# One line of a mixer's hand-written order: three state products and two ropes put elsewhere in the program

## The chip, the cores and the metric

The kernel runs on one core of one Trainium2 chip. A core has five engines, each with a queue of its own that it works through in order: TensorE (PE; its weight loads are shown apart as PEld), VectorE (DVE), ScalarE (ACT), GpSimd (POOL) and SyncE (SP), which here issues the transfers. The engines wait for one another only through semaphores. The metric is device time in microseconds (us), lower is better: 1969.81 us is the median of three runs (1968.73 to 1970.2).

## The reference, cut to what matters

Two transformer blocks run one after the other on 512 tokens of width 1024. The first is a feed-forward layer, a mixer, another feed-forward layer and a gate; the second is two layers of a recurrent mixer. The change lies in the first block's mixer alone:

```
z = rmsnorm(h, norm_mix) @ w_in
q, kc, vc, ksl, vsl, kw, vw, g, u = split(z)
q, kc, ksl, kw = rope(q), rope(kc), rope(ksl), rope(kw)
o_nsa = nsa_attention(q, kc, vc, ksl, vsl, kw, vw, sigmoid(g), ...)   # compresses kc and vc, then attends
o_s5  = s5_mixer(u, ...)                                              # a complex linear recurrence over time
h = h + concat(o_nsa, o_s5) @ w_out
```

`rope` turns pairs of values by a position's angle. `s5_mixer` runs a state-space recurrence in 32 groups of 16 channels.

## The kernel before, in words

**Weights.** All weight matrices stream from memory as one sequence of chunks of eight 128x128 blocks (class `Stream`). A chunk is loaded by SP into `wstage` (3 buffers, L82), copied by ACT into a rounded high part `whi` (L98), and DVE forms the rest as the low part `wlo` (L108). A product of a block is three matmuls (`mm3`, L145 to L147): high x high, high x input's low part, low x high. So the third matmul of a chunk is the first that needs `wlo`. The code asks for parts ahead: at the second block of a chunk it issues the `whi` of the chunk after next, at the fifth block the `wlo` of the chunk after next. Since every engine works in order, where this asking stands in the program decides what is queued ahead of it.

**The mixer's middle part.** The string `ORDER` (L668) is a list of steps that `act` carries out one by one:

- `p0` to `p7`: one projection each, 24 matmuls of 128x512, one chunk of weights (`proj`). The results of p2 and p3 are keys, those of p4 to p7 queries.
- `r0` to `r7`: what follows a projection. For all but r1 this is `rope`: four ACT copies of a quarter each out of the PSUM bank (L638), one DVE product out of the same bank (L639), and put off into the list `todo` two more DVE operations (L642, L643) and, for keys, the splitting into parts (L828, L829, and two POOL copies L830, L832).
- `v0` to `v3`: eight small matmuls into a PSUM bank (L762, "state product"), a POOL product (L765), and two put-off steps `turn` and `back`, put at the front of `todo`: the state-space chain on DVE, L772 to L784, whose fourth operation is a scan. `back` also issues the loads of the tables of the next state product (L706, L709).
- `y0` to `y3`: first everything in `todo` is emitted, then 16 small matmuls (L797, L798; L798 reads the chain's result `s5w`), ACT copy and square (L801, L652); a gelu on DVE and ACT (L655, L656, L657, L660) and its write to memory are put off into `todo`.
- `b0`, `b1`: DVE and ACT gather windows for the compression (L854 to L858); `c0` to `c7`: a quarter each of two compressions, eight matmuls of 128x256 and a whole chunk of weights in about 1 us; `t`: a transpose and a small gelu; `u`: transfers; `xN`: emit N put-off steps.

A projection emits one put-off step after every second block. So what a `v` or `r` puts off is emitted on DVE and ACT in the midst of the next projection, and the request for `wlo` at the fifth block falls between such steps.

**Banks.** Projections and state products take PSUM banks in turn from two pairs, `pa` and `pb`. A bank is free again when what reads it (L639, L772 and L774, or L950) has run.

Names used below: "chunk of p4" is the chunk of weights that projection p4 multiplies by; "chain 2" is the DVE chain of v2.

Of the kernel before, what the change touches and what calls it, by code (L numbers as in the profile page):

```python
# [664 lines left out]


PROJ = [("w_kc", 0), ("w_vc", 0), ("w_ksl", 0), ("w_kw", 0)] + [("w_q", m) for m in range(4)]
ORDER = "p0 u v0 p1 r0 r1 p2 x2 b0 y0 p3 v1 c0 r2 p4 y1 c1 v2 x2 r3 c2 r4 b1 c3 p5 y2 p6 t v3 c4 r5 p7 r6 r7 y3 c5 c6 c7"  # L668


ATT = "c0 q0 S00 D00 c1 S01 c2 T000 D01 T001 T002 S10 T010 T012 D10 c3 S11 T011 D11 T101 q1 c4 V0 T100 T102 S20 c5 D20 T110 T111 S21 T112 D21 c6 c7 V1 T201 T200 T202 S30 T210 T211 D30 T212 S31 D31 V2 y0 q2 y1 T300 T301 T302 S40 T311 T312 D40 y2 T310 S41 D41 V3 T400 T401 y3 T402 S50 T411 D50 T410 T412 S51 D51 q3 g0 V4 T500 T501 S60 T502 T511 T512 D60 T510 S61 D61 V5 g1 T601 T600 T602 S70 T611 T612 D70 T610 S71 D71 g2 T700 T702 V6 T710 T712 T711 T701 g3 V7"
# [2 lines left out]
def mixer(k, xs, norm, ins, scr, on_tile):  # L674
    nc, v = k.nc, k.nc.vector
    with ExitStack() as outer:
# [45 lines left out]
        def pump(n=1):  # L722
            for _ in range(n):
                if todo:
                    todo.pop(0)()
# [217 lines left out]
        def act(s):  # L943
            kind, n = s[0], int(s[1:] or 0)
            if kind == "p":
                C["ps", n] = proj(*PROJ[n])
            elif kind == "r":
                name, m = PROJ[n]
                if name == "w_vc":
                    v.tensor_mul(kvc[1], C["ps", n], norm.row)  # L950
                elif name == "w_q":
                    roped(C["ps", n], q[m], scale=0.125)
                else:
                    roped(C["ps", n], *((kvc[0],) if name == "w_kc" else (None, keys(int(name == "w_kw")))))
            elif kind == "u":
                u_write(3)
                u_read(1)
            elif kind == "y":
                step(n)
            elif kind == "v":  # L960
                s5_v(n)
            elif kind == "b":
                drain()
                B[n] = cmp_blocks(n)
            elif kind == "c":
                x, j = divmod(n, 4)
                C[x] = cmp_h(x, B[x], ("cmp_wk1", "cmp_wv1")[x], range(4 * j, 4 * j + 4), C.get(x))
            elif kind == "t":
                C["g"] = cmp_t(0, C[0])
            elif kind == "x":  # L970
                pump(n)
        for s in ORDER.split():
            act(s)
# [1347 lines left out]
```

## Time and profile before

| | |
|---|---|
| median of 3 runs | 1969.81 us (1968.73 to 1970.2) |
| profiled execution | 1971.62 us, of which the span is 1969.9 us |
| PE busy | 1925.6 us, 98% of the span, 9336 matmuls |
| DVE busy | 1334.8 us, 68% |
| ACT busy | 830.7 us, 42% |
| POOL busy | 157.0 us, 8% |
| load of a weight chunk | 512 KB, 3.6 us median from issue to landing, 304 of them |

The span is what the trace covers. Busy shares are averages over very different stages. The stretch that the change touches lies from about 430 to 505 us; in it the granted TensorE clock (PEclk, 1.00 is 2.4 GHz, 0.50 is 1.2 GHz) isn't always full. A row of the timeline gives the start, the duration, the engine, the line, what it writes and reads, how many, and in brackets the engine's idle time before it and who ended that.

### The profile page before, as it was taken

How to read it: one execution, taken by the hardware profiler on the slowest of the kernel's cores; microseconds unless marked ns; L12 is line 12 of the kernel's file. 1: busy time of each engine (PE TensorE's matmuls, PEld its weight loads, DVE VectorE, ACT ScalarE, POOL GpSimd, SP SyncE). 2: the span in 40 equal slices, each digit the busy share in tenths (PEclk: the TensorE clock that was granted, in tenths of full speed). 3: DMA queues.
4: the chain of work that ended last, by engine and by line, in shares of the span. 5: the costliest groups of instructions: out<-in, count | busy, mean ns of one | idle time of the engine just before them, and what ended most of it. 6: DMA issues, size and time to landing. Idle time of an engine off the chain costs nothing.

```text
span 1969.9 us, 24779 instructions
## 1 busy us (share of the span) xinstructions
PE 1925.6 (98%) x9336; PEld 1577.9 (80%) x9336; DVE 1334.8 (68%) x2189; ACT 830.7 (42%) x1252; POOL 157.0 (8%) x217
## 2 busy tenths in 40 slices
PE   8999999997999999999999999999999999999997
PEld 6888888886867888888888877888888877888886
DVE  7766666768665575666666786887774775877743
ACT  5323232435555432232234455545442455555431
POOL 1000000111144000000001100111000000101001
PEclk9999999998899999999999999999999999999999
DMA  5334445366300365656543423222343233232241
GB/s 181 100 114 156 148 150 162 116 213 187 113 1 24 102 224 183 203 174 209 172 148 99 126 86 129 75 76 75 96 149 119 86 129 97 75 92 90 75 149 55
DMA packets 102553, 244.29 MB, mean 124 GB/s; under 512 B 24601, under 2 KB 37657, under 8 KB 102433
## 3 DMA queue, kind: packets, MB, share of 16 engines
q1 hardware_dynamic: 101744, 242.01, 38.7%
q8 instruction: 73, 1.20, 0.2%
q10 hardware_dynamic: 688, 0.70, 0.1%
q14 instruction: 48, 0.39, 0.1%
HBM read 220.38 MB, written 21.10 MB: 123 GB/s over the span
## 4 chain that ended last, share of the span: by engine, by line
PE 56%; DVE 7%; ACT 3%; issue 1%; POOL 0%; DVEq 0%; ACTq 0%
PE pbsecond L145 3%; PE pbsecond L147 3%; PE pbsecond L146 3%; PE pasecond L146 3%; PE pasecond L147 3%; PE pasecond L145 3%; PE pbhead L145 2%; PE pbhead L146 2%; PE pbhead L147 2%; PE pahead L147 2%; PE pahead L145 2%; PE pahead L146 2%; PE paout L145 2%; DVE wlo L108 2%; PE paout L147 2%; PE paout L146 2%
## 5 line engine op out<-in xcount | busy, mean ns | idle before, releaser
L108 DVE TENSOR_TENSOR wlo<-wstage,whi 128x1024 fp32r<-128x1024 f32 (+1 forms) x305 | 380.1, 1253 | 71.5 <-ACT whi L98 71.0
L98 ACT ACTIVATE whi<-wstage 128x1024 fp32r<-128x1024 f32 (+1 forms) x306 | 313.9, 1044 | 114.2 <-DMA wstage<-in_wpack_dram 26.0
L303 ACT ACTIVATE t<-t 128x512 f32<-128x512 f32 x44 | 27.9, 634 | 166.1 <-DVE t L302 166.1
L145 PE MATMUL pahead<-xnh,whi 128*128 128x512 f32 x208 | 83.3, 400 | 0.0
L147 PE MATMUL pahead<-xnh,wlo 128*128 128x512 f32 x208 | 81.3, 391 | 0.9 <-DVE wlo L108 0.9
L177 POOL TENSOR_TENSOR nacc<-nacc,nsq 128x512 f32<-128x512 f32 x20 | 27.2, 1365 | 681.5 <-ACT nsq L169 681.5
L146 PE MATMUL pahead<-xnl,whi 128*128 128x512 f32 x208 | 81.0, 390 | 0.0
L145 PE MATMUL pbhead<-xnh,whi 128*128 128x512 f32 x192 | 77.7, 405 | 1.7 <-DVE zs L1581 1.7
L145 PE MATMUL pbfirst<-xnh,whi 128*128 128x512 f32 x176 | 70.8, 402 | 7.9 <-ACT whi L98 6.5
L1571 DVE SCALAR_TENSOR_TENSOR conv<-cpad,vec,conv 128x512 f32<-128x512 f32 x96 | 72.2, 752 | 5.9 <-DVE conv L1569 0.5
L146 PE MATMUL pbhead<-xnl,whi 128*128 128x512 f32 x192 | 76.0, 396 | 0.0
L147 PE MATMUL pbhead<-xnh,wlo 128*128 128x512 f32 x192 | 75.9, 395 | 0.0
L146 PE MATMUL pbfirst<-xnl,whi 128*128 128x512 f32 x176 | 69.8, 397 | 0.0
L147 PE MATMUL pbfirst<-xnh,wlo 128*128 128x512 f32 x176 | 69.5, 395 | 0.0
L145 PE MATMUL pbsecond<-xnh,whi 128*128 128x512 f32 x176 | 68.9, 392 | 0.0
L145 PE MATMUL pasecond<-xnh,whi 128*128 128x512 f32 x176 | 68.8, 391 | 0.0
L145 PE MATMUL pafirst<-xnh,whi 128*128 128x512 f32 x176 | 68.7, 390 | 0.0
L147 PE MATMUL pafirst<-xnh,wlo 128*128 128x512 f32 x176 | 68.6, 390 | 0.0
L147 PE MATMUL pbsecond<-xnh,wlo 128*128 128x512 f32 x176 | 68.6, 390 | 0.0
L146 PE MATMUL pbsecond<-xnl,whi 128*128 128x512 f32 x176 | 68.5, 389 | 0.0
L147 PE MATMUL pasecond<-xnh,wlo 128*128 128x512 f32 x176 | 68.5, 389 | 0.0
L146 PE MATMUL pafirst<-xnl,whi 128*128 128x512 f32 x176 | 68.5, 389 | 0.0
(775 smaller groups left out, 5251.8 us busy)
## 6 DMA issues: line engine op xcount, KB each, us to landing
wstage<-in_wpack_dram SPq DMA_DIRECT2D x304, 512.0 KB, 3.6
adaw<-in_wada_dram SPq DMA_DIRECT2D x48, 512.0 KB, 4.5
adaw<-in_wshift_dram SPq DMA_DIRECT2D x8, 512.0 KB, 4.9
scr_v<-vv SPq DMA_DIRECT2D x16, 256.0 KB, 2.0
vr<-scr_v SPq DMA_DIRECT2D x16, 256.0 KB, 4.6
xr<-scr_x SPq DMA_DIRECT2D x16, 256.0 KB, 5.6
h<-in_xT_dram SPq DMA_DIRECT2D x8, 256.0 KB, 6.4
s5vw<-scr_wq SPq DMA_DIRECT2D x64, 32.0 KB, 2.1
```

The costliest lines, as they stand in the source:

```text
L98: k.nc.scalar.activation(self.hi[c][:, s], self.stage[c][:, s], AF.Copy)
L108: eng.tensor_sub(self.lo[c][:, s], self.stage[c][:, s], self.hi[c][:, s].bitcast(F32))
L145: mm(ps, w[0], x[0], start=start, stop=False)
L146: mm(ps, w[0], x[1], start=False, stop=False)
L147: mm(ps, w[1], x[0], start=False, stop=stop)
L177: k.nc.gpsimd.tensor_add(self.acc[1], self.acc[1], sq)
L303: nc.scalar.activation(t1, t1, AF.Silu)
L1571: v.scalar_tensor_tensor(c, xp[:, 1 + j:1 + j + T], w(j), c, op0=OP.mult, op1=OP.add)
```

## The change

Only the order string differs. Three state products and two ropes move:

```
-ORDER = "p0 u v0 p1 r0 r1 p2 x2 b0 y0 p3 v1 c0 r2 p4 y1 c1 v2 x2 r3 c2 r4 b1 c3 p5 y2 p6 t v3 c4 r5 p7 r6 r7 y3 c5 c6 c7"
+ORDER = "p0 u v0 p1 r0 r1 p2 x2 b0 y0 v1 p3 c0 r2 p4 y1 r3 c1 v2 r4 x2 c2 b1 c3 p5 y2 v3 p6 t c4 r5 p7 r6 r7 y3 c5 c6 c7"
```

- v1 goes ahead of p3 (was behind it), v3 ahead of p6 (was behind p6 and t).
- r3 goes ahead of c1 and v2, r4 ahead of the two put-off steps (`x2`) that are chain 2.

On SP the table loads that chain 1 issues (L706, L709, the second behind chain 1's reads of the old table) now stand ahead of one weight load and of the write of y0, where they stood behind both; POOL's order is unchanged. The amount of work is the same; the banks are handed out in another sequence (p3 now takes `pa`, v1 `pb`).

On DVE, behind the compression windows of b0 (the last of them is L858) and up to p4's low part: the difference, + for the order now and - for the order before.

```order
+L772 TENSOR_TENSOR s5r_3737<-pbmix,s5R 128x512
+L774 TENSOR_TENSOR s5r_3738<-pbmix,s5R 64x512 x2
+L775 TENSOR_TENSOR s5r_3737<-s5r_3737,s5r_3738 128x512
+L776 SCALAR_TENSOR_TENSOR s5r_3738<-s5rho,s5r_3737 128x512
+L781 TENSOR_TENSOR s5w_3736<-s5r_3738,s5R 128x8x63
+L783 TENSOR_TENSOR s5r_3737<-s5r_3738,s5R 64x512 x2
+L784 TENSOR_TENSOR s5w_3736<-s5w_3736,s5r_3737 128x8x63
+L108 TENSOR_TENSOR wlo<-wstage,whi 128x1024
 L655 TENSOR_SCALAR s5gw<-s5gw 128x512
 L656 TENSOR_TENSOR s5gw<-s5gw,s5yg 128x512
 L660 SCALAR_TENSOR_TENSOR s5yg<-s5gw,s5yg 128x512
-L108 TENSOR_TENSOR wlo<-wstage,whi 128x1024
```

Chain 1 (L772 to L784) now stands ahead of the low part of p4's chunk and of the gelu of y0; before, both stood ahead of the chain. In the same way chain 3 now stands ahead of the gelu of y2 and the low part of p7's chunk.

On ACT, behind y1 (L801 and L652): r3 and r4 are the four-copy groups L638; the first L98 is the high part of c3's chunk, the second that of p5's.

```order
 L801 ACTIVATE s5yg<-pc 128x512
 L652 ACTIVATE s5gw<-s5yg 128x512
+L638 ACTIVATE ropeb<-pamix 32x512 x4
 L98 ACTIVATE whi<-wstage 128x1024
 L638 ACTIVATE ropeb<-pbmix 32x512 x4
 L98 ACTIVATE whi<-wstage 128x1024
-L638 ACTIVATE ropeb<-pbmix 32x512 x4
 L657 ACTIVATE s5gw<-s5gw 128x512
```

Both groups moved one place forward: r3's copies are ahead of c3's high part, r4's ahead of p5's.

On DVE in the same place: the end of chain 2 as it stood, and what now stands ahead of it. The L108 with a + and the one behind the first L639 are low parts of c2's and c3's chunk, in that order.

```order
-L781 TENSOR_TENSOR s5w_3916<-s5r_3918,s5R 128x8x63
-L783 TENSOR_TENSOR s5r_3917<-s5r_3918,s5R 64x512 x2
-L784 TENSOR_TENSOR s5w_3916<-s5w_3916,s5r_3917 128x8x63
-L639 SCALAR_TENSOR_TENSOR ropeo<-pbmix,ropet 128x512
+L108 TENSOR_TENSOR wlo<-wstage,whi 128x1024
+L639 SCALAR_TENSOR_TENSOR ropeo<-pamix,ropet 128x512
 L108 TENSOR_TENSOR wlo<-wstage,whi 128x1024
 L639 SCALAR_TENSOR_TENSOR q_3314<-pbmix,ropet 128x512
+L772 TENSOR_TENSOR s5r_3924<-pamix,s5R 128x512
+L774 TENSOR_TENSOR s5r_3925<-pamix,s5R 64x512 x2
+L775 TENSOR_TENSOR s5r_3924<-s5r_3924,s5r_3925 128x512
+L776 SCALAR_TENSOR_TENSOR s5r_3925<-s5rho,s5r_3924 128x512
```

The first operations of r3 and r4 (both L639) moved ahead of chain 2; the low part of p5's chunk follows chain 2 directly, as before except for the L639 of r3 that stood between.

## Rows read from the trace of the kernel before

**Rows 1.** Waits of PE in the mixer: who for whom, total us, times, longest.
```profile
PE pbmix L145 <- DVE ropeo L639: 5.9, 1, 5.9
PE pc L798 <- issue: 4.1, 2, 2.6
PE pamix L147 <- DVE wlo L108: 1.7, 1, 1.7
```

**Rows 2.** Stretches: length, busy PE, PEld, DVE, ACT, POOL, PEclk, DMA, GB/s.
```profile
444.00:457.00 13.00, 11.53 (x71) 11.30 (x71) 9.81 (x13) 6.14 (x10) 3.65 (x4) 0.74 0.60 179
503.00:517.00 14.00, 13.97 (x109) 13.80 (x110) 9.52 (x17) 5.98 (x10) 0.00 (x0) 1.00 0.68 198
```

**Rows 3.** Timeline of DVE from b0 to c7's low part.
```profile
434.35 0.67 DVE L858 TENSOR_TENSOR cAh<-cA,cAh 128x496 fp32r<-128x496 f32 x1 [0.69 <-ACT cAh L857]
...
438.10 1.22 DVE L108 TENSOR_TENSOR wlo<-wstage,whi 128x1024 fp32r<-128x1024 f32 x1
439.24 0.69 DVE L772 TENSOR_TENSOR s5r<-pamix,s5R 128x512 f32<-128x512 f32 x1
...
446.13 1.22 DVE L108 TENSOR_TENSOR wlo<-wstage,whi 128x1024 fp32r<-128x1024 f32 x1
...
454.23 1.23 DVE L108 TENSOR_TENSOR wlo<-wstage,whi 128x1024 fp32r<-128x1024 f32 x1 [2.02 <-ACT whi L98]
455.82 0.69 DVE L772 TENSOR_TENSOR s5r<-pamix,s5R 128x512 f32<-128x512 f32 x1 [0.36 <-PE pamix L762]
...
463.32 1.22 DVE L108 TENSOR_TENSOR wlo<-wstage,whi 128x1024 fp32r<-128x1024 f32 x1
...
465.05 0.42 DVE L655 TENSOR_SCALAR s5gw<-s5gw 128x512 f32<-128x512 f32 x1
...
480.93 0.68 DVE L858 TENSOR_TENSOR cAh<-cA,cAh 128x496 fp32r<-128x496 f32 x1 [0.69 <-ACT cAh L857]
482.08 0.43 DVE L655 TENSOR_SCALAR s5gw<-s5gw 128x512 f32<-128x512 f32 x1 [0.47 <-ACT s5gw L652]
...
484.55 1.22 DVE L108 TENSOR_TENSOR wlo<-wstage,whi 128x1024 fp32r<-128x1024 f32 x1
...
497.90 1.28 DVE L639 SCALAR_TENSOR_TENSOR q<-pamix,ropet 128x512 f32<-128x512 f32 x2
...
501.76 3.49 DVE L108 TENSOR_TENSOR wlo<-wstage,whi 128x1024 fp32r<-128x1024 f32 x3
```

**Rows 4.** Timeline of PE: p4, y1, c1; p5, y2, p6; p7; c7.
```profile
439.37 0.50 PE L147 MATMUL pbmix<-xnh,wlo 128*128 128x512 f32 x1
...
444.52 0.33 PE L797 MATMUL pc<-U,s5T 128*128 128x64 f32 x2
...
451.71 0.55 PE L871 MATMUL pc<-whi,cAh 128*124 128x256 f32 x1
...
464.59 0.79 PE L147 MATMUL pbmix<-xnh,wlo 128*128 128x512 f32 x1
...
471.28 0.33 PE L797 MATMUL pc<-U,s5T 128*128 128x64 f32 x2
...
474.77 0.48 PE L145 MATMUL pamix<-xnh,whi 128*128 128x512 f32 x1
...
485.82 0.50 PE L147 MATMUL pamix<-xnh,wlo 128*128 128x512 f32 x1 [1.68 <-DVE wlo L108]
...
503.03 0.38 PE L872 MATMUL pc<-wlo,cAh 128*124 128x256 f32 x1 [0.37 <-DVE wlo L108]
```

**Rows 5.** Timeline of ACT: after y1, and the high part of c5's chunk.
```profile
453.16 1.04 ACT L98 ACTIVATE whi<-wstage 128x1024 fp32r<-128x1024 f32 x1
454.22 2.40 ACT L638 ACTIVATE ropeb<-pbmix 32x512 f32<-32x512 f32 x4
...
486.48 1.05 ACT L98 ACTIVATE whi<-wstage 128x1024 fp32r<-128x1024 f32 x1
```

**Rows 6.** Timeline of SP's queue: the tables for v2.
```profile
445.52 0.89 SPq L709 DMA_DIRECT2D s5R<-scr_R  x2
```

## The prediction

> **What bounds the kernel now.** I read the list of waits first. In the mixer PE waits in three places worth the name [rows 1]: 5.9 us before p5 (its bank is held by r3's L639), 4.1 us in two pieces before the L798 of y1 (1.5) and y3 (2.6), both for a state-space chain, and 1.7 us at p7 for a low part of weights. The change aims at the first two kinds: v1 and v3 one projection sooner, r3 ahead of chain 2. Then the stretches by clock: after the short wait at y1 the clock falls, and over 444 to 457 us it averages 0.74 [rows 2], so 26% of 13 us, 3.4 us, is lost to 1.2 GHz beside the wait itself. So the three waits, 11.7 us, carry a surcharge.
>
> But the timelines of PE and DVE, side by side, say who sets the pace. Of DVE's time from 434 to 503 us little is free, and when PE has done c5 and c6 it waits again, for c7's low part [rows 4]. That low part leaves DVE at 501.76 [rows 3], PE uses it 1.27 us later, and from there to 517 PE is busy 13.97 of 14 us at full clock [rows 2]. So what counts is when DVE gets to c7's low part; PE's earlier waits are partly a picture of that queue.
>
> **The change, followed along DVE.** All times are of the profiled execution; "+" is against the same event before. Up to b0's last window operation, L858 at 434.35 [rows 3], nothing that DVE or ACT does has moved; it ends near 435.0.
>
> *v1 ahead of p3.* Chain 1 took 439.24 to 446.13, 6.89 us [rows 3]. It can now start at 435.0, since v1 directly follows y0 on PE, and ends at 441.9. y1 was at 444.52 [rows 4], so its 1.5 us wait goes. But p4's low part is now queued behind the chain: it ran at 438.10 and runs at 441.9. PE's third matmul of p4 came 1.27 us after it (439.37 [rows 4]); now 443.2, **+3.8 us**. PE wants p4 no later than before, because v1 and p3 only swap. Behind that matmul all of PE waits: the rest of p4, y1, c1, v2. The wait removed at y1 comes back larger, one projection earlier, with another releaser.
>
> From there the rest of p4 is 5.15 us (439.37 to 444.52) and y1 at full clock 3.49 (like y2, 471.28 to 474.77) [rows 4]: y1 ends at 451.8, against 451.71. If the 3.8 us idle brings the clock down as the 1.5 us did, 3.4 us more [rows 2]: 455.2. I take that, since the longer waits before p5 and y3 were also followed by the lower clock, and only 1.7 us at p7 was not. So y1's end, called E, is **+3.5 us**, with +0.1 as the other bound.
>
> ACT meanwhile stands at the tanh of y0's gelu until chain 1 is through, and r2's copies and c2's high part come behind it (to about 449), which E covers. SP now keeps one weight load behind the tables for v2, which wait for the chain's last reads: they were issued 6.28 us after its start (445.52 [rows 6], 439.24), now about 441.3, so that load goes at 442.2, lands 3.6 later at 445.8 by the page's median, and its copy is not due before 448. Cost nothing; if a landing took over 6 us, each us more would be one on c2.
>
> *r3 and r4 ahead of chain 2.* Before, chain 2 started at 455.82, E + 4.1, as soon as v2 was done, and p5's low part at 463.32, E + 11.6 [rows 3, 4]. Now L639 of r3 and r4 precede it, and each follows its four copies on ACT. ACT reaches this work at E + 1.45 (453.16, behind y1's copy and square): copies 2.40, c3's high part 1.06, copies 2.40 [rows 5], then L639, 0.6 (two took 1.28 [rows 3]): the chain starts at E + 7.9, **3.8 us later after E**, and p5's low part at E + 14.8. The bank is no longer what p5 waits for, but its low part is, 3.2 us later after E. With E: 470.0 against 463.32, **+6.7 us**. Queued behind on DVE: the gelu of y1, the rests of r3 and r4, low parts of p6 and c4, both windows of b1.
>
> By the Trainium skill, "PSUM — Partial Sum Buffer", section "PSUM bank collisions raise a hardware error", two engines may not read one bank in the same quadrant at a time, ACT and DVE included, and software must keep them apart; that speaks against this change. No run here shows what happens otherwise; the trace merely never has an L639 beside its own copies, since before it always came long after. If L639 need not wait, chain 2 would start about 1.3 us sooner and the ropes r2 and r7 give 0.6 each, so the sum below would be 2.5 us less.
>
> *v3 ahead of p6.* p5's low part to the gelu of y1 is now 1.14 us (the L639 between has gone), and from that gelu (465.05) to the end of b1's windows (480.93 + 0.6) 16.5 us pass [rows 3]: 487.6. There the gelu of y2 stood; now chain 3 does, 6.89 us, and p7's low part follows at 494.5, against 484.55: **+10 us**, and PE's third matmul of p7 at 495.8 against 485.82. PE, which has p5, y2, v3, p6 and c4 behind it by about 492, waits 3 to 5 us here instead of 1.7. y3 finds its chain done; its 2.6 us goes.
>
> *Down to c7.* Before, p7's low part to c7's was 17.2 us with chain 3 in it. Now the chain is out, the gelu of y2 (2.47, 482.08 to 484.55) is in, but ACT is late: under chain 3 it used to do c5's and c6's high parts and the copies of r5, r6, r7; now it gets to them only after that gelu. 1.14 + 2.47, + 0.79 to c5's high part (486.48 [rows 5], counted from 484.55 + 1.14), + 2 x 1.06 + 3 x 2.40 = 9.32, + 3.26 from r7's L639 to c7's low part (501.76 - 497.90 = 3.86 less one L639 of 0.6) = 17.0 us. So c7's low part is at 511.5: **+9.8 us**. PE is at c7 by about 506 to 510, so DVE still decides. The rest, PE busy without a gap, is shifted whole.
>
> **Sum.** +3.5 (p4's low part behind chain 1, less the wait at y1, with the clock) + 3.2 (copies ahead of chain 2) + 3.3 (chain 3 ahead of p7's low part, less the gelu, less one L639) - 0.2 = +9.8 us. The profiled execution took 1971.62 us, 1.8 more than the median; on the median 1969.81 + 9.8 = **1979.6 us**. Own range 1977 to 1982.
>
> **Rivals.** *The clock holds in p4* (for it: 1.7 us of idle at p7 left it at full; against it: 1.5 at y1 did not). Then E is +0.1 and the sum +6.4: 1976.2.
>
> *The clock falls once more behind c7.* PE now waits some 3 us or more before c7, which was 0.4, and the projections behind it, so far at 1.00, lose up to 3.4: +13.2, 1983.0.
>
> *DVE swallows it.* If ACT's copies cost less delay than I count (L639 free of them, or the copies finding gaps), and the clock holds, 6.4 - 2.5 = +3.9 or less remains; with one part of the order better than I think, no change can be told: about 1971.5.
>
> *Faster: PE's own waits are the bound.* The place is p4's third matmul; the price is all that the change names, 5.9 + 4.1 = 10.0 us, so 1959.8. It decides from the point where p4's low part starts by about 438, as it did. For it: the list of waits names bank and chain, and DVE does have gaps, 2.0 us before c3's low part, 0.4 before chain 2 [rows 3], that would close. Against it: the queue puts 6.89 us ahead of that low part.
>
> **How the numbers follow.** Two runs of this kernel can be told apart at about 0.2%, 3.9 us. Forecast +9.8: 0.50. Clock holds, +6.4: 0.18. Clock once more, +13.2: 0.12. Swallowed, within 3.9 us: 0.11. Faster: 0.09. So slower by over 0.2% 0.80, within 0.11, faster 0.09. The range 1970 to 1984 leaves out the faster case (0.09) and some of the two at its ends.
>
> **What the profile after would show.** Right: PE's wait list has low parts (DVE L108) at p4 (near 4 us), p5 (over 6) and p7 (3 to 5) and no L639; the low clock lies in p4 and y1 at about 443 to 450; chain 1 starts at 435, chain 2 about 8 us after y1's end, behind L639 of r4; ACT's tanh of y0's and y2's gelu waits over 6 us each. Wrong: p4's low part before 439, or chain 2 within 5 us of y1's end, or p7's third matmul before 490, or c7 unmoved although p5 is late.

## The result, and the profile after

The changed kernel took 1984.38 us (median of 3 runs, 1982.33 to 1985.65) against 1969.81: a ratio of 1.0070, 95% interval 1.0056 to 1.0084. A second set of five runs gave 1982.77 against 1970.04, ratio 1.0061 (1.0048 to 1.0073). So the change costs 12 to 14 us. The forecast was 9.8 more.

The profiled execution has a span of 1980.6 us, 10.7 more than the one before. The two executions already differ ahead of the change: the last window operation of b0 starts at 434.35 in the trace before [rows 3] and at 433.23 after, and between 431.9 and 433.3 in every other kernel profiled here. So I compare stretches that begin at that operation, not spans.

The waits of TensorE in the mixer (columns as in [rows 1]):

```profile
PE pbmix L147 <- DVE wlo L108: 10.1, 2, 6.4
PE pamix L147 <- DVE wlo L108: 6.7, 1, 6.7
PE pc L871 <- ACT whi L98: 3.0, 2, 1.8
PE pc L872 <- DVE wlo L108: 2.8, 2, 1.9
```

The bank (5.9) and the chains (4.1) of [rows 1] are gone, and low parts stand in their place: 3.7 and 6.4 us at p4 and p5 and 6.7 at p7. Smaller waits at c3 and c7, half of them for high parts, add 5.8 us. VectorE's timeline, the rows that answer to [rows 3]:

```profile
433.23 0.68 DVE L858 TENSOR_TENSOR cAh<-cA,cAh 128x496 fp32r<-128x496 f32 x1 [0.69 <-ACT cAh L857]
433.83 0.68 DVE L772 TENSOR_TENSOR s5r<-pbmix,s5R 128x512 f32<-128x512 f32 x1
...
440.72 1.22 DVE L108 TENSOR_TENSOR wlo<-wstage,whi 128x1024 fp32r<-128x1024 f32 x1
...
455.95 0.69 DVE L639 SCALAR_TENSOR_TENSOR ropeo<-pamix,ropet 128x512 f32<-128x512 f32 x1 [3.93 <-ACT ropeb L638]
457.03 1.23 DVE L108 TENSOR_TENSOR wlo<-wstage,whi 128x1024 fp32r<-128x1024 f32 x1 [0.39 <-ACT whi L98]
459.45 0.69 DVE L639 SCALAR_TENSOR_TENSOR q<-pbmix,ropet 128x512 f32<-128x512 f32 x1 [1.19 <-ACT ropeb L638]
460.06 0.68 DVE L772 TENSOR_TENSOR s5r<-pamix,s5R 128x512 f32<-128x512 f32 x1
...
466.94 1.22 DVE L108 TENSOR_TENSOR wlo<-wstage,whi 128x1024 fp32r<-128x1024 f32 x1
...
486.71 0.69 DVE L772 TENSOR_TENSOR s5r<-pamix,s5R 128x512 f32<-128x512 f32 x1 [2.83 <-PE pc L882]
...
493.61 1.22 DVE L108 TENSOR_TENSOR wlo<-wstage,whi 128x1024 fp32r<-128x1024 f32 x1
...
510.65 3.49 DVE L108 TENSOR_TENSOR wlo<-wstage,whi 128x1024 fp32r<-128x1024 f32 x3
```

From top to bottom: chain 1 directly behind the windows, p4's low part behind it, the two ropes that wait for their copies on ScalarE (with c3's low part between them), chain 2, p5's low part, chain 3 (its wait of 2.83 us was not foreseen), p7's low part, c7's.

How much of this is work and how much is standing still? The stretch from b0's last window operation to c7's low part, before and after (columns as in [rows 2], so VectorE is the third number behind the length):

```profile
434.35:501.76 67.41, 55.82 (x305) 49.60 (x304) 57.52 (x81) 39.35 (x61) 6.92 (x8) 0.85 0.60 181
433.23:510.65 77.42, 55.47 (x302) 46.99 (x300) 57.31 (x80) 40.33 (x62) 6.92 (x8) 0.84 0.52 157
```

VectorE is busy 57.5 us before and 57.3 after. All of the 10.0 us by which the stretch grew is its idle time, 9.9 us before and 20.1 after. By the brackets of its timeline, stops of L639 for its own copies, of which there were none here before, come to 9.6 us and the stop of chain 3 to 2.8; its other stops are 2.2 us shorter together.

TensorE in the same places, and the first attention matmul behind c7:

```profile
441.99 0.79 PE L147 MATMUL pbmix<-xnh,wlo 128*128 128x512 f32 x1 [3.66 <-DVE wlo L108]
...
452.02 0.36 PE L871 MATMUL pc<-whi,cAh 128*124 128x256 f32 x1
...
468.22 0.79 PE L147 MATMUL pbmix<-xnh,wlo 128*128 128x512 f32 x1 [6.45 <-DVE wlo L108]
...
486.11 0.55 PE L882 MATMUL pc<-ii,cH 124*128 124x64 f32 x4
...
494.88 0.79 PE L147 MATMUL pamix<-xnh,wlo 128*128 128x512 f32 x1 [6.75 <-DVE wlo L108]
...
511.93 0.58 PE L872 MATMUL pc<-wlo,cAh 128*124 128x256 f32 x1 [1.88 <-DVE wlo L108]
...
528.64 1.56 PE L1014 MATMUL pc<-kcmp,q 128*128 128x64 f32 x13
```

Each long wait is followed by the lower clock, as these stretches show (columns as in [rows 2]):

```profile
442.00:444.00 2.00, 2.00 (x5) 1.61 (x6) 1.27 (x3) 0.96 (x2) 0.00 (x0) 0.50 0.94 290
446.00:457.00 11.00, 9.93 (x76) 9.25 (x74) 4.92 (x6) 7.97 (x12) 3.65 (x4) 1.00 0.52 136
460.00:472.00 12.00, 5.01 (x11) 3.51 (x12) 10.92 (x16) 1.15 (x3) 0.00 (x0) 0.50 0.58 215
492.00:499.00 7.00, 4.12 (x10) 3.25 (x11) 5.22 (x10) 2.33 (x5) 0.00 (x0) 0.56 0.06 9
510.00:516.00 6.00, 4.12 (x19) 4.08 (x19) 5.46 (x9) 1.87 (x3) 0.00 (x0) 0.50 0.50 144
516.00:530.00 14.00, 14.00 (x112) 14.00 (x111) 6.61 (x15) 7.68 (x14) 0.00 (x0) 0.98 0.65 194
```

At p5 the clock had fallen already ahead of the long wait: it is 0.50 from 458.7 to 461.7, behind two waits of 1.12 and 0.88 us at c3. The last two rows answer to the second of [rows 2]: the stretch behind c7's low part, at 1.00 before, now begins with 6 us at 1.2 GHz.

### The profile page after: what moved, and what is told of

Read it like the earlier page. It is cut to its first block, busy times and chain, and to the rows that moved or that the text cites. A ratio compares the mean times of both kernels' runs of the same rounds, so it can differ in the third digit from the quotient of the medians.

```text
span 1980.6 us, 24779 instructions
## 1 busy us (share of the span) xinstructions
PE 1925.5 (97%) x9336; PEld 1576.4 (80%) x9336; DVE 1334.5 (67%) x2189; ACT 829.3 (42%) x1252; POOL 157.8 (8%) x217
## 4 chain that ended last, share of the span: by engine, by line
PE 57%; DVE 6%; ACT 3%; issue 1%; POOL 0%; DVEq 0%; ACTq 0%
PE pbsecond L145 3%; PE pbsecond L147 3%; PE pbsecond L146 3%; PE pasecond L146 3%; PE pasecond L147 3%; PE pasecond L145 3%; PE pbhead L145 2%; PE pbhead L146 2%; PE pbhead L147 2%; PE pahead L147 2%; PE pahead L145 2%; PE pahead L146 2%; PE paout L145 2%; PE paout L146 2%; PE paout L147 2%; PE pbgates L145 2%
## 5 line engine op out<-in xcount | busy, mean ns | idle before, releaser
L108 DVE TENSOR_TENSOR wlo<-wstage,whi 128x1024 fp32r<-128x1024 f32 (+1 forms) x305 | 381.6, 1257 | 71.5 <-ACT whi L98 70.9
L98 ACT ACTIVATE whi<-wstage 128x1024 fp32r<-128x1024 f32 (+1 forms) x306 | 313.6, 1043 | 113.6 <-DMA wstage<-in_wpack_dram 23.6
```

The costliest lines, as they stand in the source:

```text
L98: k.nc.scalar.activation(self.hi[c][:, s], self.stage[c][:, s], AF.Copy)
L108: eng.tensor_sub(self.lo[c][:, s], self.stage[c][:, s], self.hi[c][:, s].bitcast(F32))
```

## The experiments

Two theories. **A**: what VectorE has to do between b0 and c7, with its stops for ScalarE, sets the pace; TensorE's waits only picture that queue. **B**: the price is what stands behind a chain, so that TensorE finds it late. The table gives, for each kernel, the stretch from b0's last window operation to c7's low part and to the first attention matmul, in its own trace, as the difference from before (67.41 and 83.44 us), beside the ratio of times with its interval and what that is of 1970 us.

| kernel | to c7's low part | to attention | ratio | us |
|---|---|---|---|---|
| changed, first runs | +10.0 | +12.0 | 1.0070 (1.0056 to 1.0084) | +13.8 |
| changed, again | +10.8 | +13.1 | 1.0061 (1.0048 to 1.0073) | +12.0 |
| v1 alone | +0.9 | +2.3 | 1.0007 (0.9998 to 1.0017) | +1.4 |
| r3 and r4 alone | +2.5 | +2.5 | 1.0015 (1.0006 to 1.0025) | +3.0 |
| v3 alone | +4.8 | +6.2 | 1.0032 (1.0020 to 1.0044) | +6.3 |
| v1, r3 and r4 | +5.3 | +5.3 | 1.0030 (1.0019 to 1.0040) | +5.9 |
| changed, low parts early | +8.2 | +10.2 | 1.0050 (1.0038 to 1.0062) | +9.9 |
| changed, low parts on GpSimd | +5.9 | +8.2 | 1.0037 (1.0024 to 1.0051) | +7.3 |
| v1, low parts on GpSimd | +2.9 | +3.2 | 1.0013 (1.0004 to 1.0022) | +2.6 |
| before, low parts on GpSimd | +2.6 | +2.6 | 1.0011 (1.0002 to 1.0019) | +2.2 |
| before, r3 and r4 finished late | -4.8 | -0.7 | 1.0002 (0.9991 to 1.0013) | +0.4 |
| changed, r3 and r4 finished late | +10.7 | +14.3 | 1.0097 (1.0084 to 1.0110) | +19.1 |
| before, four ropes finished late | -5.9 | +1.4 | 1.0027 (1.0017 to 1.0038) | +5.3 |

Where the third column and the last agree, the time lies in this stretch. They differ by over 3 us in two kernels, of which more below.

### The parts one by one

```
e1  -... y0 p3 v1 c0 ...             +... y0 v1 p3 c0 ...
e2  -... y1 c1 v2 x2 r3 c2 r4 b1 ... +... y1 r3 c1 v2 r4 x2 c2 b1 ...
e3  -... y2 p6 t v3 c4 ...           +... y2 v3 p6 t c4 ...
e11 the first two of these together
```

> Only v1 is moved ahead of p3; r3, r4 and v3 stay where they were. My account (DVE's queue): p4's low part stands behind chain 1, PE waits 3.7 us at p4's third matmul, the wait at y1 goes, and the sum is +2 to +3.5 us (the first term of the forecast, less what DVE catches up in the 4 us for which it stands before c3's low part). Rival (the ropes' or v3's place alone does it, v1 is harmless since it removes a wait): within 1 us of before, or up to 3 us faster.

> Only r3 and r4 are moved ahead of chain 2; v1 and v3 stay. My account (the ropes' copies on ACT hold up chain 2 and with it p5's low part): the bank wait before p5 goes, a wait of about 6 to 7 us for p5's low part comes, +2.5 to +3.2 us in all. Rival (the bank was what p5 waited for): p5 starts up to 6 us earlier, the sum is -3 us or better.

> Only v3 is moved ahead of p6 and t; v1, r3 and r4 stay. My account: the wait at y3 (2.6 us) goes, the one at p7's third matmul grows from 1.7 to about 5 us, ACT gets to the copies of r5 to r7 late, +3 to +4 us. Rival (the chain was what y3 and the rest waited for): -2.6 us.

> The changed kernel with v3 back behind t: v1 ahead of p3, r3 and r4 ahead of chain 2 only. If the parts add: 2.3 + 2.5 us by the traces of the two parts alone (from b0's last window operation to the first attention matmul), so +4 to +5.5 us over the kernel before, 6.5 to 9 us under the changed kernel. If v3's place costs so much only because p5 and y2 are already late: nearer to the changed kernel, +7 or more over before.

The ropes alone cost what was expected. v1 alone costs less by the times (1.4 us, where 2 to 3.5 were expected): y1's end comes only 1.45 us later in its trace, not 3.5, and VectorE catches up 0.5 of that before chain 2, which no longer stops for v2's product (0.36 us [rows 3]). It does not catch up in the gap before c3's low part, which grew from 2.02 us to 2.49. Of the 2.3 us at the first attention matmul 1.4 arise behind c7, where TensorE now stops for 1.96 us (0.37 before [rows 4]). v3 alone costs 6.2 us where 3 to 4 were expected. The parts very nearly add: 2.3 + 2.5 + 6.2 = 11.0 against 12.0 and 13.1 together, and 4.8 against 5.3 without v3. About half of the loss is v3's. In the trace of v3 alone:

```profile
481.50 0.69 DVE L772 TENSOR_TENSOR s5r<-pamix,s5R 128x512 f32<-128x512 f32 x1 [1.80 <-PE pc L882]
488.40 1.22 DVE L108 TENSOR_TENSOR wlo<-wstage,whi 128x1024 fp32r<-128x1024 f32 x1
```

Chain 3 stands idle for t's matmul, whose result it does not read. In the built program its first result, `s5r1`, lies at the address that `cH` had, the tile that t's matmul reads: both come from the ring of nine buffers that the helper `sc` (L698) hands out. v3 now stands ahead of p6, t still behind it. So chain 3 cannot start until p6 and t are through, however early v3 is, while what was queued behind it on VectorE (the gelu of y2, p7's low part) waits with it. In four kernels the chain starts 0.59 or 0.60 us after that matmul (changed 486.71 and 486.11; again 487.35 and 486.76; v3 alone 481.50 and 480.91; changed with ropes late 487.46 and 486.86). In the other two kernels with v3 ahead of p6 (low parts early, and low parts on GpSimd in the changed kernel) VectorE comes to it 2.6 and 2.1 us after that matmul and does not stop. A larger ring was not tried, so the buffer is shown by addresses and times, not by an experiment of its own.

### The low parts elsewhere

```
e4  in s5_v, from the second product on:
+            if b:
+                k.ws.split(k.ws.pos // CH + 3)
e5, e6, e8  in low_piece, for the chunks of p4, p5 and p7:
-        eng = k.nc.gpsimd if c == 1 and s.start else k.nc.vector
+        eng = k.nc.gpsimd if c == 1 and s.start or c in self.onpool else k.nc.vector
```

> The changed order, but at each of v1, v2, v3 the high and low part of the chunk of p4, p5, p7 are asked for ahead of the chain. Theory 1 (the low parts' place behind the chains is the loss): the waits at p4, p5 and p7 go and with them most of the loss; the time is that of before or better, up to 10 us below the changed kernel. Theory 2 (the pace is that of DVE's whole list down to c7, with its stops for ACT; where a low part stands only says where PE notices): the three waits go too, but others come in their place (c2, c3, p6, c5 to c7), c7's low part leaves DVE when it did, and the time is that of the changed kernel within 2 us.

> The changed kernel, with the low parts of the weight chunks of p4, p5 and p7 (128x1024 subtractions, 1.22 us each on VectorE) formed by GpSimd in place of VectorE: the three low parts for which TensorE waits longest no longer stand behind a chain. Theory A (VectorE's whole list sets the pace, TensorE's waits are its picture): the list loses 3 x 1.2 = 3.7 us of work and the stops of p4, p5 and p7 no longer slow TensorE's clock, but the copies ahead of chain 2 and all other low parts stay: 4 to 7 us under the changed kernel, still 2 to 8 us over the kernel before, with TensorE's waits at p4, p5 and p7 gone and others, for low parts that VectorE forms, at c5 to c7. Theory B (what costs is that a low part stands behind a chain): all of the changed kernel's loss returns, 10 us or more under it, at or under the kernel before. Rival C (GpSimd's operations slow VectorE's beside them; in the trace 128x512 operations of VectorE took 0.98 to 1.10 us beside GpSimd's instead of 0.69): the gain is eaten, within 2 us of the changed kernel. An estimate for a low part on GpSimd, from its 1.3 us for a 128x512 operation, is 2.7 us.

> The kernel before with v1 ahead of p3 alone, and the low parts of the chunks of p4, p5 and p7 formed by GpSimd. Theory A: v1's early chain no longer delays p4's low part, TensorE waits neither for it nor for y1's chain, and VectorE's list is 3.7 us shorter: 3 to 6 us under the kernel before. Theory B: the waits at p4 and y1 go, 1.5 to 4 us; the same sign. Rival C: GpSimd's operations slow VectorE's beside them by as much as they take off: within 2 us of the kernel before.

> The kernel before with its own order, and the low parts of the chunks of p4, p5 and p7 formed by GpSimd. Theory A: VectorE's list between b0 and c7's low part is 3.7 us shorter, part of it ahead of a stop for ScalarE where it gains nothing: 1 to 4 us under the kernel before, with the waits for y1's and y3's chains as they were or little shorter (the chains start up to 1.2 us sooner). Theory B: no low part there stands behind a chain but p7's, whose wait is 1.7 us: 0 to 2 us under. Rival C: GpSimd slows VectorE: 0 to 3 us over.

Theories 1 and 2 of the first expectation are B and A. With the low parts ahead of the chains (e4), the three long waits are down from 16.8 to 1.5 us and others have come. Its longest waits of TensorE:

```profile
PE pc L874 <- DVE wlo L108: 4.9, 4, 2.1
PE pc L873 <- ACT whi L98: 3.8, 2, 2.5
PE pc L799 <- ACT cy L886: 3.5, 1, 3.5
```

The time came down by 2 to 4 us, not 12: theory B falls, as far as the low parts go. TensorE even ends y1 13.8 us behind b0's windows, 3.6 sooner than in the kernel before, and c7's low part still leaves VectorE 8.2 us late.

On GpSimd they bring the changed kernel 4 to 6 us, within theory A's range, but the other two kernels stand 2 to 3 us over the one before where theory A has them 1 to 6 under. And in none of the three was VectorE's list shorter: from b0's last window operation to c7's low part VectorE is busy 57.9 us in the changed kernel with low parts on GpSimd (57.3 without), 59.5 in v1 (57.5) and 58.9 in the kernel before (57.5), although three operations of 1.22 us are gone. The three stretches in that order:

```profile
433.03:506.34 73.31, 56.99 (x302) 47.45 (x300) 57.90 (x77) 40.33 (x62) 14.03 (x11) 0.84 0.54 166
432.54:502.88 70.34, 57.57 (x297) 49.65 (x296) 59.47 (x78) 39.28 (x61) 14.63 (x11) 0.83 0.57 173
431.92:501.90 69.98, 54.90 (x308) 49.03 (x307) 58.94 (x78) 39.30 (x61) 16.11 (x13) 0.84 0.60 175
```

VectorE and then GpSimd, in v1 with low parts on GpSimd:

```profile
433.83 1.39 DVE L775 TENSOR_TENSOR s5r<-pbmix,s5R 64x512 f32<-64x512 f32 x2
435.26 2.51 DVE L776 TENSOR_TENSOR s5r<-s5r,s5r 128x512 f32<-128x512 f32 x1
437.87 1.22 DVE L777 TENSOR_TENSOR_SCAN s5r<-s5rho,s5r 128x512 f32<-128x512 f32 x1
```

```profile
434.83 2.39 POOL L109 TENSOR_TENSOR wlo<-wstage,whi 128x1024 fp32r<-128x1024 f32 x1 [5.70 <-ACT whi L99]
```

The addition of the chain with both inputs in SBUF, elsewhere 0.69 us, took 2.51: it ends 0.55 us after GpSimd's subtraction (437.22). The multiplication ahead of it, with one input in PSUM, ran beside GpSimd at its usual length. In the Trainium skill, "SBUF — State Buffer", section "Who interferes with whom", such an addition contends with a GpSimd instruction that reads SBUF, and the one that comes second is blocked; the trace agrees, with 1.8 us for one low part that would have taken VectorE 1.2. So rival C (GpSimd's work slows VectorE's) held for the list in all three kernels. What the changed kernel gained all the same was idle time of VectorE, 20.1 us down to 15.4: with TensorE's stops for these low parts down to 1.7 us or less, y1 ended 5.3 us sooner and t's matmul came 2.1 us ahead of chain 3, whose stop of 2.83 us went, and the stop for r3's copies fell from 3.93 to 2.09. The other two kernels had no such stops to lose.

### Work taken out of VectorE's list

```
e9, e10  put-off halves of r3 and r4, into a list of their own, with buffers of their own
+        todo[0:0] = late[::-1]          (behind the last step of ORDER)
e12      those of r3, r4, r6 and r7
+        todo[:] = late[1:2] + todo + late[2:] + late[:1]
```

> The kernel before in its own order; the put-off halves of r3 and r4 (two VectorE operations of each rope, r3's split into parts with its GpSimd copies) run behind c7's low part instead of between p5's and p6's low parts, from buffers of their own. In the trace of before they stand from 467.50 to 472.26 us, 4.8 us of VectorE's list, and TensorE waits for none of them. Theory A (VectorE's list from b0 to c7 sets the pace): p7's low part, chain 3 and c7's low part come some 4 us sooner, TensorE's waits at p7 (1.7) and y3 (2.6) shrink, and the whole is 2 to 4.5 us under the kernel before (less if the put-off work delays a low part behind c7). Theory B (what costs is what stands behind a chain, or which bank is held): no chain, low part or bank has changed its place, so within 1 us of before.

> The changed kernel with the put-off halves of r3 and r4 behind c7's low part in the same way. In its trace chain 3 stands idle for 2.8 us before its start since TensorE, at the lower clock through p5, comes late with v3's product. Theory A in its plain form (the list alone): 4 to 5 us under the changed kernel. Theory A with the clock (after the long wait at p5 the pace of the middle part is TensorE's, at 1.2 GHz): chain 3 starts no sooner, its idle time grows to 5 us or more, and the gain is 0 to 2 us.

> The kernel before in its own order; the put-off halves of r3, r4, r6 and r7 run behind c7's low part, those of r6, r7 and r3 also behind the gelu of y3. With r3's and r4's alone put off, c7's low part came 4.8 us sooner after b0, but the time did not move: TensorE now waited 2.9 us at c7 (0.4 before) and ran at 1.2 GHz behind it, which gave 4.2 us back before the first attention matmul. Here 2.7 us of VectorE's work ahead of c7's low part go too, so the wait at c7 is 1 us or less, held by ScalarE's high part. If it was the stop at c7 with its lower clock that ate the gain: no lower clock behind c7, and 3 to 5.5 us under the kernel before. If what ate it is the work that was put off (low parts late behind c7): within 1.5 us of the kernel before, with TensorE's waits behind c7 grown.

In the kernel before, c7's low part came 4.8 us sooner, all that was taken out of the list, as theory A has it. The time did not move by the ratio; the twelve runs fall in two groups, seven at 1966.8 to 1969.83 us and five at 1974.02 to 1976.76, where 21 of the 23 of the kernel before lie at 1967.45 to 1972.92. In its trace the first attention matmul is 0.7 us sooner. TensorE at c7, and the stretch around and behind it:

```profile
496.75 0.57 PE L878 MATMUL pc<-wlo,cAh 128*124 128x256 f32 x1 [2.92 <-DVE wlo L108]
```

```profile
494.00:498.00 4.00, 1.25 (x6) 1.25 (x7) 3.97 (x6) 1.40 (x2) 0.00 (x0) 0.81 0.20 55
498.00:502.00 4.00, 4.00 (x19) 4.00 (x19) 3.46 (x7) 1.44 (x2) 0.00 (x0) 0.50 0.91 301
```

TensorE had gained more than VectorE, waited 2.9 us for c7 in place of 0.4 [rows 4], and ran on at 1.2 GHz; behind the put-off work it waited another 0.87 us for a low part. From c7's low part to attention it took 20.2 us in place of 16.0. With r6 and r7 late as well (e12) that wait is 0.9 us and the clock holds, as expected of the stop:

```profile
498.00:502.00 4.00, 3.37 (x27) 3.38 (x27) 3.89 (x8) 1.70 (x2) 0.00 (x0) 1.00 0.77 279
510.00:514.00 4.00, 0.22 (x1) 0.22 (x2) 3.00 (x5) 2.19 (x3) 1.42 (x2) 0.97 0.94 332
```

But the work that was put off now stands ahead of a copy that TensorE needs at the end of the projection: the second row's idle time belongs to one wait of 4.84 us for it. Both causes that were named are thus real, the time (+5.3 us) is neither of those expected, and neither version beats the kernel before; putting r3's half off behind that copy was not tried.

In the changed kernel the same 4.8 us less did nothing for c7's low part (+10.7), as expected with the clock:

```profile
487.46 0.69 DVE L772 TENSOR_TENSOR s5r<-pamix,s5R 128x512 f32<-128x512 f32 x1 [6.41 <-PE pc L888]
```

Chain 3 starts no sooner, its idle time grows from 2.83 to 6.41 us, and it still starts behind t's matmul. Theory A in its plain form falls here: ahead of chain 3 the pace is TensorE's, through p5's late start and low clock, v3, p6 and t. The time, expected 0 to 2 us under the changed kernel's, was 5 to 7 over it: 1.3 to 1.6 us of this arise between c7's low part and attention, the rest far behind the change (last section).

The changed kernel itself was run once more beside those with low parts on GpSimd:

> The changed kernel once more, beside the others on one chip: by the traces +10 to +11 us over the kernel before, by the medians of the first runs +14.6. The delay at c7's low part was 10.0 us in the trace and everything behind it shifted whole, so +10 to +12 us is expected; if +14 or more returns, some 3 to 4 us lie in executions that the trace did not catch.

It gave 12.0 us by the ratio, at the upper end of what was expected.

## Why the prediction was right, and where not

The time moved the way that was forecast, by 12 to 14 us and not 9.8; both medians, 1984.38 and 1982.77, lie above the prediction's own range of 1977 to 1982. The terms, each from the two timelines (before from [rows 3, 4]):

| from, to | before | after | difference | forecast |
|---|---|---|---|---|
| b0's windows, y1's end (E) | 17.36 | 18.79 | +1.4 | +3.5 |
| E, p5's low part | 11.61 | 14.92 | +3.3 | +3.2 |
| p5's low part, p7's | 21.23 | 26.67 | +5.4 | +3.3 |
| p7's low part, c7's | 17.21 | 17.04 | -0.2 | -0.2 |
| c7's low part, attention | 16.03 | 17.99 | +2.0 | 0 |

**First term: mechanism right, size too large.** p4's third matmul came 8.76 us after b0's windows against 5.02, 3.7 later (3.8 forecast). The surcharge for the clock, taken as 3.4 us from [rows 2], was 1.4: y1 followed p4 without a second stop, and by 446 the clock was full.

**Second term: right, by its own steps.** Chain 2 starts 8.0 us after E (7.9 forecast), p5's low part 14.9 (14.8). L639 stops for its copies, 3.93 and 1.19 us, although it reads nothing that they write, and these stops carry the term. By the Trainium skill, "PSUM — Partial Sum Buffer", section "PSUM bank collisions raise a hardware error", software must keep two engines' reads of one bank apart; the trace agrees so far that no L639 runs beside its own copies.

**Third term: the step that failed** is "There the gelu of y2 stood; now chain 3 does". It took for granted that chain 3 is ready when VectorE comes to it. It waited 2.83 us for t's matmul, for its buffer, behind a p5 that came late and ran at half clock (7.04 us from its third matmul to y2, where p4 took 5.15 [rows 4]; by that, an estimate, 1.9 of the 2.83 us are the clock's). b1's windows gave 0.8 back: their last addition took 0.57 us, where before it took 1.35 beside a GpSimd product. The wait at p7 was 6.75 us instead of 3 to 5. The stop could have been seen: the prediction has TensorE through c4, one step behind t, by about 492, and chain 3 ready to start at 487.6.

**Fourth term: right.** The stops for ScalarE that it counts are there.

**Behind c7: the rival "the clock falls once more"** came true, cheaper: waits of 1.84 and 1.88 us at c7 and 0.50 from 510 to 516 cost 2.0 us, not 3.4.

So the sum at c7's low part, +10.0 against +9.8, is right by luck in part: two errors cancel (-2.1 and +2.1). What the times show beyond it is the last row, and in the first runs up to 1.8 us more that their trace does not have. That "DVE still decides" at c7 held; that it decides everywhere did not: ahead of chain 3 it is TensorE.

## What to carry to other kernels

A step that is moved ahead takes its place in a ring of buffers with it: look which tile had the buffer before, and whether its reader still stands behind. Where an engine's queue is full, moving a step to meet one wait hands the wait to whatever the step overtakes; count what is overtaken, not what is met. And work taken off the engine that seems to set the pace pays only until the next engine stops, and a stop that lowers TensorE's clock can give nearly the whole gain back (4.2 of 4.8 us here). Before handing work to another engine, look at what will run beside it: busy time of VectorE did not fall when GpSimd took three of its operations.

## What the runs showed that I had not expected

The lower clock does not follow from the wait alone. In the next stage of the kernel, far behind the change, all kernels have the same wait of 0.4 us in front of eight matmuls of one column. Some 5 us behind it the changed kernel runs at full clock, and the one with r3 and r4 late at half. The changed kernel, then that one:

```profile
1134.78 1.02 PE L192 MATMUL pm<-ones,nacc 128*128 128x1 f32 x8 [0.38 <-DVE nacc L182]
1140.00:1144.00 4.00, 4.00 (x22) 3.26 (x21) 3.18 (x13) 0.60 (x1) 0.00 (x0) 1.00 0.01 4
```

```profile
1137.08 1.02 PE L192 MATMUL pm<-ones,nacc 128*128 128x1 f32 x8 [0.38 <-DVE nacc L182]
1142.00:1146.00 4.00, 4.00 (x15) 3.62 (x16) 1.56 (x10) 0.00 (x0) 0.00 (x0) 0.50 0.01 2
```

Summed over 10 us stretches between 900 and 1400 us, the share of the clock that is not granted comes to 10.2 us in that kernel and in the one with four ropes late, and to 3.4 in every other trace here. These are the two whose times stand over their stretch: from the first attention matmul to the end of the span they take 1457.4 and 1456.5 us, all others 1450.1 to 1452.6. All five runs of the former lie between 1988.59 and 1991.0 us, which speaks against an accident of one execution. Steps of about that size also stand between runs of one kernel (with r3 and r4 late, above; with v1, r3 and r4, eight runs at 1972.55 to 1975.97 us and three at 1980.61 to 1981.01), but no trace caught one, so whether they are this clock is not shown. What decides it stays open.
